# Two places for the weights in their buffers, by whether TensorE loads or streams them

## The chip, the cores and the metric

The kernel runs on one core of a Trainium2 chip. The metric is the device time of one execution in microseconds (us); several runs are taken and their median is told. One further execution was recorded by the hardware profiler, and the rows below come from it.

## What is computed

A trunk of two layers over 512 positions of 1024 channels, float32. Each layer: a normalisation, one input projection to 3072 columns that feeds three mixers (a gated linear recurrence in both directions, a two-dimensional Fourier transform, windowed attention with three dilations), one output projection with a residual, a second normalisation and an MLP with a squared ReLU and 4096 inner columns.

```
def reference(x, positions, attn_norm_w, w_in, hgrn_lower_bounds, w_out, mlp_norm_w, w_up, w_down, final_norm_w):
    ...
    for layer in range(DEPTH):
        h = rms_norm(x, attn_norm_w[layer])
        proj = h @ w_in[layer]
        a_q, a_i, a_zf, a_zb, a_g, b_u, c_q, c_k, c_v = jnp.split(proj, SPLIT_POINTS, axis=-1)
        ...
        mixed = jnp.concatenate([o_a, o_b, o_c], axis=-1)
        x = x + mixed @ w_out[layer]
        h = rms_norm(x, mlp_norm_w[layer])
        x = x + jnp.square(jax.nn.relu(h @ w_up[layer])) @ w_down[layer]
    return rms_norm(x, final_norm_w)
```

## The kernel before

**The dense products.** Every dense product is done in three passes over rounded halves. A float32 operand a is split into a high part ah (rounded to fewer bits, type fp32r) and the rest al; the product is ah·bh + ah·bl + al·bh (`mac3`, line 366). So each 128-row slice of the contraction costs three matmuls, each with its own load of a 128x128 stationary operand. In the profile such a matmul is two rows: a PEld LDWEIGHTS (the *loaded* operand, 128 columns per partition) and a PE MATMUL (the *streamed* operand, 512, 256 or 258 columns per partition). The load of the next matmul runs beside the streaming of the present one.

**Which operand is loaded.** In most products the weight is loaded and the activation streams, 512 columns at a time: the input projections `in…` through `proj_T` (line 439), the output projection `wo…`, the MLP's first product `up…` and, in layer 0, its second `dn…`. Where the result is wanted with positions on the partitions, the roles are turned round: the activation is loaded and the weight streams, 256 columns at a time (`proj_tok`, line 446). That holds for the weights of the recurrence's values (`in…_6`, `in…_7`), of the attention's values (`in…_18` to `in…_21`) and of the MLP's second product in layer 1 (`dt…`). The second Fourier step streams a constant matrix (`fc…`) in pieces of 258 columns against loaded activations.

**The weights.** `prefetch` (line 335) takes the next weight of a fixed list: SyncE's DMA brings 512 KB into a raw buffer, ScalarE rounds it into `wh` (line 351), VectorE subtracts for `wl` (line 352). For `fc` two DMAs of GpSimd's queue fill `wh` and `wl` directly. There are two buffers of each, 1152 float32 wide, of which 1024 (1032 for `fc`) are used, from the buffer's start.

**Where the operands lie.** The allocator places every pool's buffers one behind the other in a partition. All buffers that hold an operand of a dense matmul are multiples of 512 bytes long: `wh` and `wl` 4608, `xh` and `xl` (normalised activations) 16384, the pool `g` (MLP activations `ma`, mixer outputs `mix`, Fourier operands `fu` and `fab`) 4096. Each of them starts 32 bytes past a multiple of 512. A loaded operand is a slice of 128 columns, that is 512 bytes; slices start at multiples of 512 bytes from the buffer's start, streamed ones too. So the place of a loaded operand less that of a streamed one, modulo 512 bytes, is the same for all of these matmuls: 0. In this text that difference is called the *offset*. Two small groups differ. The first Fourier step streams its matrix `d` from a buffer that starts 192 bytes past a multiple of 512, against activations at 32: its offset is −160 (48 matmuls of 256 columns). The second step streams `fc` in pieces of 1032 bytes: its offsets are 0, −8, −16 and −24 in turn (96 matmuls of 258 columns).

**The order of the work.** The order of TensorE's instructions is written out: `ORDER` (line 38) gives, letter by letter, which stream issues next, and `weave` and `scripted` (lines 162 to 198) pin it; behind the end of that text a table of estimated clocks decides. In the MLPs and the output projections only one stream is left, and the matmuls follow one another.

Of the kernel before, what the change touches and what calls it, by code (L numbers as in the profile page):

```python
# [14 lines left out]
FR = mybir.dt.float32r  # L15
# [11 lines left out]
P = 128  # L27
# [10 lines left out]
ORDER = ("mr13mn7mng13mhmr6mhomh7mj6mhj4mhj7mhj9mhmj6m2hjh2mj4mh2mj2mh6mj2mh2mj6mj7mj5mj12mS3mS2T4mT2mT2mSVT2m3TVTST2m2T3mVS3T5mTVS4TVS2T2m2TVS2m2T2m2T2mVmTmT4mT2mT4mV35m",  # L38
         "11mnmn7mgmh6mh8moh9mh4mj3mj3mh3mjh6mjh4mj3mh9mj2h4mjmh6mh2mjmh6mj4mj4mj7mj6mj10mS6mS3m2T3mTmT2mVSTm2T3mTmVST4mTm2TVS4TVS4TSVTm3TmVS2m4T2mV3m2T5m2TmV40m")
HP = 400  # L40
RANK = "gonrxhjam"
DEEP = 2
START = "ho{}1"
# [76 lines left out]
class Trunk:  # L120
# [59 lines left out]
    def weave(self, streams, order=""):  # L180
# [4 lines left out]
        while live or self.fresh:  # L185
            for k in list(self.fresh):
                live[k] = [self.fresh.pop(k), 0.0]
            live = {k: live[k] for k in sorted(live, key=RANK.index)}
            times = {k: self.evt.get(w, 1e9) if isinstance(w, str) else w for k, (_, w) in live.items()}
# [123 lines left out]
    def weight_order(self):  # L313
# [18 lines left out]
                            o.append((w["w_dt"][hf, q, c], f"dt{l}_{hf}{q}{c}"))  # L332
        return o

    def prefetch(self, after=(None,)):
        nc = self.nc
        if not self.wlist:
            return
        src, name = self.wlist.pop(0)
        h = self.buf("wh", [P, 1152], f"wh_{name}", FR)  # L340
        l = self.buf("wl", [P, 1152], f"wl_{name}", FR)
        if isinstance(src, int):
            nc.gpsimd.dma_start(h[:, 0:4 * COLD], self.t["c_d2"][2 * src])
            nc.gpsimd.dma_start(l[:, 0:4 * COLD], self.t["c_d2"][2 * src + 1])
        else:
            raw = self.buf("wraw", [P, 1024], f"wr_{name}")
            n = 1024 // len(after)
            for i, then in enumerate(after):
                cs = slice(i * n, (i + 1) * n)
                nc.sync.dma_start(raw[:, cs], src[:, cs])  # L350
                nc.scalar.activation(h[:, cs], raw[:, cs], AF.Copy)  # L351
                nc.vector.tensor_tensor(l[:, cs], raw[:, cs], h[:, cs].bitcast(F32), op=OP.subtract)  # L352
                if then:
                    then()
        self.wnext.append((name, h, l))
# [122 lines left out]
    def hgrn_gates(self, layer, p, zq, zz):  # L478
# [4 lines left out]
        if p:  # L483
            yield f"kp{layer}0"
        with self.tc.high_priority(offset=HP):
            qn = self.buf("th", [P, S], f"hqn{layer}{p}")
# [56 lines left out]
    def hgrn_levels(self, layer, p):  # L543
# [25 lines left out]
        for lv in range(7):  # L569
# [26 lines left out]
            if lv > 0:  # L596
# [4 lines left out]
                te = tot.rearrange("p (n e) -> p n e", e=2)  # L601
            with self.tc.high_priority(offset=HP):
                for z, odd, lo in ((k, 0, 0), (k, 1, 64), (q, 1, 0), (q, 0, 64)):
# [368 lines left out]
    def mlp(self, layer):  # L972
# [7 lines left out]
        for half in range(2):  # L980
# [8 lines left out]
            if last:  # L989
# [7 lines left out]
                for q in range(4):  # L997
                    def ev(it, ps, q=q):
# [3 lines left out]
                        if half == 1:  # L1002
# [3 lines left out]
                            if q == 3:  # L1006
                                with self.tc.high_priority(offset=HP):
                                    r = self.final_scale(it, st)
# [132 lines left out]
```

## Time and profile before

| what | us |
|---|---|
| runs: median of 3 | 1297.52 |
| runs: lowest and highest | 1297.07, 1298.42 |
| profiled execution, its own time | 1296.64 |
| span of its instructions | 1294.9 |

The mean granted clock of TensorE over the span is 0.995 of its full 2.4 GHz. The profile gives times of instructions by engine: PE is the matmul, PEld the load of its stationary operand, DVE is VectorE, ACT ScalarE. A matmul's recorded duration holds the way of its last column through the array, so that successive matmuls overlap in the record; what one costs in a dense stretch is the distance from its start to the next one's start. It is got from a row that merges n matmuls: (length of the row less the duration of one) divided by n − 1, or from a piece of the chain of waits, whose length over its count gives it directly. In the chain, which is followed back from the last instruction, a piece is a stretch in which one engine's instructions set the end.

### The profile page before, as it was taken

To read this page: it belongs to the slowest core of one execution; us is meant where nothing else is said; L and a number is where in the kernel's file an instruction comes from. 1 tells how busy PE (TensorE), PEld (TensorE's weight loads), DVE (VectorE), ACT (ScalarE), POOL (GpSimd) and SP (SyncE) were. 2 spreads that over 40 slices of the span, in tenths; PEclk is the share of its full clock that TensorE was granted. 3 is DMA by queue.
4 is the path that set the end of the run, shared out by engine and by line. 5 is a ranking of instruction groups with operands and counts; after the bars stand their busy time and mean duration, and the time that the engine had idled before them with its cause. 6 is when DMAs were issued, how large, how long until landed. Compare 5 with 4: busy or idle time off the path is not lost.

```text
span 1294.9 us, 22041 instructions
## 1 busy us (share of the span) xinstructions
PE 1247.0 (96%) x9344; PEld 1071.1 (83%) x9344; DVE 705.0 (54%) x1314; ACT 538.2 (42%) x855; POOL 32.7 (3%) x54
## 2 busy tenths in 40 slices
PE   7799999899999999999999999889999999999997
PEld 6788877788888888888878987668888999888997
DVE  7798686554442234433369868765455322444234
ACT  6744265644442124433355335574344311344222
POOL 2100000000000000100010000000000000000000
PEclk9999999999999999999999999999999999999999
DMA  6321222142232222233322212304322232223221
GB/s 225 98 71 47 82 81 76 58 131 89 98 98 98 98 98 98 98 98 130 114 92 90 68 66 81 92 10 145 106 83 92 89 98 88 94 97 112 99 87 76
DMA packets 36498, 121.42 MB, mean 94 GB/s; under 512 B 4192, under 2 KB 5040, under 8 KB 36400
## 3 DMA queue, kind: packets, MB, share of 16 engines
q1 hardware_dynamic: 33120, 110.46, 25.8%
q0 software_dynamic: 2848, 7.98, 2.2%
q8 instruction: 73, 1.20, 0.4%
q10 hardware_dynamic: 432, 1.57, 0.3%
q14 instruction: 25, 0.20, 0.1%
HBM read 114.24 MB, written 4.72 MB: 92 GB/s over the span
## 4 chain that ended last, share of the span: by engine, by line
PE 85%; DVE 6%; ACT 5%; issue 2%; DMA 0%; SPq 0%; ACTq 0%; DVEq 0%
PE mm_up L144 27%; PE mt_dt L144 14%; PE md L144 13%; PE mm_in L144 11%; PE mo L144 7%; PE mt_cv L144 3%; PE ao L144 2%; PE at_tr L160 1%; PE sc L144 1%; ACT at L765 1%; PE mt_hi L144 1%; DVE hy L606 1%; ACT pt L779 1%; DVE wl_in L352 1%; PE f L144 1%
## 5 line engine op out<-in xcount | busy, mean ns | idle before, releaser
L144 PE MATMUL mt_dt<-wh_dt,ma 128*128 128x256 f32 x1024 | 144.3, 283 | 0.0
L144 PEld LDWEIGHTS mt_dt<-wh_dt,ma 128*128 128x128 f32 x1024 | 132.5, 192 | 0.2
L144 PE MATMUL mm_up<-xh,wl_up 128*128 128x512 f32 x512 | 130.1, 391 | 0.0
L965 DVE SCALAR_TENSOR_TENSOR mr<-mm_up,rb 128x512 f32<-128x512 f32 x64 | 44.1, 691 | 157.8 <-PE mm_up L144 149.9
L144 PE MATMUL mm_up<-xl,wh_up 128*128 128x512 f32 x512 | 129.7, 390 | 0.0
L144 PE MATMUL mm_up<-xh,wh_up 128*128 128x512 f32 x512 | 129.0, 390 | 0.0
L144 PE MATMUL md<-ma,wh_dn 128*128 128x512 f32 x512 | 121.3, 389 | 0.0
L351 ACT ACTIVATE wh_up<-wr_up 128x1024 fp32r<-128x1024 f32 x64 | 67.9, 1061 | 126.0 <-PE mm_up L144 100.8
L144 PEld LDWEIGHTS md<-ma,wh_dn 128*128 128x128 f32 x512 | 96.2, 188 | 19.9
L144 PEld LDWEIGHTS mm_up<-xh,wh_up 128*128 128x128 f32 x512 | 95.9, 188 | 19.8
L144 PEld LDWEIGHTS mm_up<-xl,wh_up 128*128 128x128 f32 x512 | 95.9, 188 | 19.7
L144 PEld LDWEIGHTS mm_up<-xh,wl_up 128*128 128x128 f32 x512 | 95.8, 188 | 19.7
L352 DVE TENSOR_TENSOR wl_dt<-wr_dt,wh_dt 128x1024 fp32r<-128x1024 f32 x32 | 39.2, 1224 | 98.6 <-ACT wh_dt L351 98.6
L352 DVE TENSOR_TENSOR wl_up<-wr_up,wh_up 128x1024 fp32r<-128x1024 f32 x64 | 78.0, 1218 | 21.4 <-ACT wh_up L351 19.1
L351 ACT ACTIVATE wh_dt<-wr_dt 128x1024 fp32r<-128x1024 f32 x32 | 33.9, 1060 | 124.1 <-PE mt_dt L144 101.3
L144 PE MATMUL mm_in<-xh,wh_in 128*128 128x512 f32 x288 | 77.8, 398 | 5.8 <-ACT xh L402 5.8
L144 PE MATMUL mt_dt<-wl_dt,ma 128*128 128x256 f32 x512 | 82.5, 283 | 0.0
L144 PE MATMUL mm_in<-xl,wh_in 128*128 128x512 f32 x288 | 78.2, 401 | 0.7 <-DVE xl L403 0.7
L351 ACT ACTIVATE wh_dn<-wr_dn 128x1024 fp32r<-128x1024 f32 x32 | 33.9, 1061 | 107.1 <-PE md L144 90.5
L967 ACT ACTIVATE mr<-mr 128x512 f32<-128x512 f32 x64 | 40.4, 632 | 88.4 <-DVE mr L965 88.3
L144 PE MATMUL mm_in<-xh,wl_in 128*128 128x512 f32 x288 | 76.3, 397 | 0.0
L144 PEld LDWEIGHTS mt_dt<-wl_dt,ma 128*128 128x128 f32 x512 | 70.8, 192 | 0.0
(229 smaller groups left out, 1988.3 us busy)
## 6 DMA issues: line engine op xcount, KB each, us to landing
wr_up<-in_w_up SPq DMA_DIRECT2D x64, 512.0 KB, 3.5
wr_in<-in_w_in SPq DMA_DIRECT2D x47, 512.0 KB, 3.5
wr_dn<-in_w_dn SPq DMA_DIRECT2D x32, 512.0 KB, 3.4
wr_dt<-in_w_dt SPq DMA_DIRECT2D x32, 512.0 KB, 3.5
wr_wo<-in_w_out SPq DMA_DIRECT2D x16, 512.0 KB, 3.7
wh_fc<-in_c_d POOLq DMA_DIRECT2D x4, 516.0 KB, 3.8
wl_fc<-in_c_d POOLq DMA_DIRECT2D x4, 516.0 KB, 4.3
x_in<-in_x SPq DMA_DIRECT2D x8, 256.0 KB, 5.7
```

Source lines behind the costliest of these rows:

```text
L144: return self.queue(self.nc.tensor.matmul(out, a, b, **kw))
L160: self.queue(self.nc.tensor.transpose(out, a, ident))
L351: nc.scalar.activation(h[:, cs], raw[:, cs], AF.Copy)
L352: nc.vector.tensor_tensor(l[:, cs], raw[:, cs], h[:, cs].bitcast(F32), op=OP.subtract)
L606: v.tensor_tensor(dst, dst, te[lo:lo + 64, :, 1 - odd, None].to_broadcast([64, nb, blk]), op=OP.mult)
L765: nc.scalar.activation(tt, tt, AF.Exp, bias=st4[:, 1:2], accum_out=st4[:, 2:3])
L779: nc.scalar.activation(pt, tr.rearrange("p (a b) -> p a b", b=P), AF.Copy)
L965: nc.vector.scalar_tensor_tensor(r, ps, 0.0, self.rb, op0=OP.max, op1=OP.mult)
L967: nc.scalar.activation(r, r, AF.Square)
```

## The change

A weight that TensorE streams is put 8 elements (32 bytes) behind its buffer's start, a weight that is loaded 120 elements (480 bytes). With buffers that start at 32 modulo 512, a loaded weight then starts at 0 modulo 512 and a streamed one at 64; the activations stay at 32. The offset becomes −32 for all dense matmuls that had 0, and −32, −40, −48 and −56 for the second Fourier step. The first Fourier step keeps −160.

```diff
 HP = 400
+PLACE = (120, 8)
 RANK = "gonrxhjam"
...
+    def streamed(self, name):
+        part, n = name.split("_")
+        return part[:2] in ("dt", "fc") or part[:2] == "in" and int(n) in (6, 7, 18, 19, 20, 21)
+
     def prefetch(self, after=(None,)):
         nc = self.nc
         if not self.wlist:
             return
         src, name = self.wlist.pop(0)
-        h = self.buf("wh", [P, 1152], f"wh_{name}", FR)
-        l = self.buf("wl", [P, 1152], f"wl_{name}", FR)
+        first = PLACE[self.streamed(name)]
+        h = self.buf("wh", [P, 1152], f"wh_{name}", FR)[:, first:]
+        l = self.buf("wl", [P, 1152], f"wl_{name}", FR)[:, first:]
```

The built programs of before and after hold the same 11,211 instructions in the same order on every engine, with the same waits and the same buffers at the same addresses. Only start addresses differ: of one operand in 5,760 less 48 matmuls that use a weight buffer, of the output of 193 roundings on ScalarE, of operands and output of 193 subtractions on VectorE, and of the targets of 8 DMAs of GpSimd's queue.

## Rows read from the trace of the kernel before

**Rows 1.** The page's busy times: engine, us, share of the span, instructions.
```profile
PE 1247.0 (96%) x9344; PEld 1071.1 (83%) x9344; DVE 705.0 (54%) x1314; ACT 538.2 (42%) x855; POOL 32.7 (3%) x54
```
**Rows 2.** The chain of waits: shares of the span by engine and line.
```profile
by line: PE mm_up L144 26.9%; PE mt_dt L144 14.2%; PE md L144 13.4%; PE mm_in L144 10.7%; PE mo L144 6.7%; PE mt_cv L144 3.4%; PE ao L144 2.1%; issue 1.9%; PE at_tr L160 1.3%; PE sc L144 1.1%; ACT at L765 1.0%; PE mt_hi L144 1.0%; DVE hy L6
```
**Rows 3.** Long pieces of that chain: start us, length us, what, count.
```profile
387.23 87.04 PE md L144 x384
...
1015.74 92.15 PE mt_dt L144 x768
```
**Rows 4.** Busy time of each engine in a stretch of layer 0's MLP.
```profile
345.00:530.00 185.00, 185.00 (x818) 153.28 (x817) 69.76 (x79) 58.90 (x71) 0.00 (x0) 1.00 0.29 97
```
**Rows 5.** Groups of matmuls and loads: shapes, count, busy us, mean ns, idle before.
```profile
L144 PE MATMUL mt_dt<-wh_dt,ma 128*128 128x256 f32 x1024 | 144.3, 283 | 0.0
...
L144 PE MATMUL mm_up<-xh,wl_up 128*128 128x512 f32 x512 | 130.1, 391 | 0.0
...
L144 PE MATMUL md<-ma,wh_dn 128*128 128x512 f32 x512 | 121.3, 389 | 0.0
...
L144 PE MATMUL mt_dt<-wl_dt,ma 128*128 128x256 f32 x512 | 82.5, 283 | 0.0
...
L144 PE MATMUL mm_in<-xh,wl_in 128*128 128x512 f32 x288 | 76.3, 397 | 0.0
...
L144 PE MATMUL md<-ma,wl_dn 128*128 128x512 f32 x256 | 63.2, 389 | 0.0
L144 PE MATMUL mo<-mix,wh_wo 128*128 128x512 f32 x256 | 63.2, 393 | 1.6 <-ACT mix L686 1.6
...
L144 PE MATMUL mo<-mix,wl_wo 128*128 128x512 f32 x128 | 32.6, 390 | 0.0
L144 PE MATMUL mt_cv<-wl_in,xh 128*128 128x256 f32 x128 | 21.6, 291 | 0.0
...
L144 PE MATMUL mt_hi<-wl_in,xh 128*128 128x256 f32 x64 | 11.1, 297 | 0.0
```
**Rows 6.** Timeline of PE in the first Fourier step (offset −160): start, length, what, count.
```profile
225.51 1.33 PE L144 MATMUL f<-d,fu 128*128 128x256 f32 x10
...
235.92 1.35 PE L144 MATMUL f<-d,fu 128*128 128x256 f32 x10
...
861.07 1.10 PE L144 MATMUL f<-d,fu 128*128 128x256 f32 x8
```
**Rows 7.** Timeline of PE in a short stretch of 256-column matmuls at offset 0.
```profile
688.87 0.64 PE L144 MATMUL mt_hi<-wh_in,xl 128*128 128x256 f32 x4
...
692.23 0.64 PE L144 MATMUL mt_hi<-wh_in,xh 128*128 128x256 f32 x4
```
**Rows 8.** All matmuls of the two Fourier steps: duration ns lowest, median, highest.
```profile
L144 PE MATMUL f<-wh_fc,fab x64: 277/283/388, 238.1 to 875.2; 128*128 128x258 f32 x64
L144 PE MATMUL f<-d,fu x48: 277/281/388, 225.3 to 862.1; 128*128 128x256 f32 x48
```
**Rows 9.** Timeline of PE in the second Fourier step (offsets 0 to −24).
```profile
871.08 1.15 PE L144 MATMUL f<-wh_fc,fab 128*128 128x258 f32 x8
...
873.41 1.12 PE L144 MATMUL f<-wh_fc,fab 128*128 128x258 f32 x8
```
**Rows 10.** Timeline of PE, transposes of 128 columns with a load each.
```profile
101.79 1.06 PE L160 MATMUL hk<-misc,hy 128*128 128x128 f32 x8 [1.58 <-DVE hy L606]
```
**Rows 11.** The same transposes: duration ns lowest, median, highest.
```profile
L160 PE MATMUL hk<-misc,hy x32: 272/273/328, 101.8 to 749.3; 128*128 128x128 f32 x32
```

## The prediction

> **What bounds the kernel now.** I read the busy times first: TensorE's matmul row is busy 1247 of 1294.9 us, VectorE 54%, ScalarE 42% [rows 1]. A matmul's recorded time overlaps the next one's, so this says only that TensorE is hardly ever without work. What sets the end is in the chain of waits: dense matmuls hold 26.9% (`mm_up`), 14.2% (`mt_dt`), 13.4% (`md`), 10.7% (`mm_in`), 6.7% (`mo`), 3.4% (`mt_cv`) and 1.0% (`mt_hi`) of the span, 76.3% together [rows 2]. In the MLP the other engines are far from it: in 185 us of layer 0, TensorE is busy throughout, VectorE for 69.76 us and ScalarE for 58.90 us [rows 4]. A dense matmul that becomes cheaper therefore shortens the kernel there one for one.
>
> What one matmul costs comes from two long pieces of the chain [rows 3]: 87.04 us for 384 matmuls of 512 columns is 226.67 ns each; 92.15 us for 768 of 256 columns is 119.99 ns each. The difference, 106.68 ns for 256 columns, is 0.4167 ns a column, one column per cycle at the full 2.4 GHz, which is also the clock granted there (1.00) [rows 4]. The streaming of 512 columns is thus 213.3 ns and that of 256 is 106.7 ns, and both leave the same rest: 13.3 ns per matmul, 32 cycles. This rest is all that a change of addresses can win where matmuls stand back to back. It doesn't grow with the columns streamed, so it belongs to the one load that each matmul has beside it.
>
> **The change part by part.** Nothing is moved, added or removed on any engine's queue; only start addresses change. There are four things to price.
>
> *The dense matmuls, offset 0 to −32.* First how many lie on the path. A share of the chain times 1294.9 us, over the cost of one, gives the matmuls that count:
> `mm_up` 348.3 us / 226.67 ns = 1537 (of 3 x 512 in [rows 5]);
> `md` 173.5 us = 765 (of 512 + 256); `mo` 86.8 us = 383 (of 256 + 128); `mm_in` 138.6 us = 611 (of 3 x 288).
> These have 512 columns: 3296. With 256 columns, at 119.99 ns: `mt_dt` 183.9 us = 1532 (of 1024 + 512), `mt_cv` 44.0 us = 367 (of 3 x 128), `mt_hi` 12.9 us = 108 (of 3 x 64): 2007. Together 5303. The rest of `mm_in`, `mt_cv` and `mt_hi` lies in the mixers beside chains of VectorE and ScalarE that end later, and I count nothing for it.
>
> Next what offset −32 does to one of them. No matmul of this kernel has that offset, so the trace bounds it by its neighbours. Offset −160, a multiple of 32 as −32 is: the first Fourier step, 256 columns. Three rows [rows 6] with a median duration of 281 ns [rows 8] give (1.33 − 0.28) / 9 = 117 ns, (1.35 − 0.28) / 9 = 119 ns and (1.10 − 0.28) / 7 = 117 ns; together 2.94 us over 25 steps, 117.6 ns: 2.4 ns under offset 0. That these stretches are short doesn't explain it: a stretch at offset 0 of about the same kind goes from 688.87 to 692.23 in 28 steps, 120.0 ns each [rows 7]. So the rest of 13.3 ns does depend on addresses, at least in part. Offsets 0 to −24 in turn, 258 columns: the second Fourier step. Its two rows [rows 9], with a median of 283 ns [rows 8], give (1.12 − 0.283) / 7 = 119.6 ns and (1.15 − 0.283) / 7 = 123.9 ns, where 258 columns with the rest of offset 0 would take 107.5 + 13.3 = 120.8. So there the rest is once 1.2 ns less and once 3.1 ns more. The bounds of the unknown are then: the whole 13.3 ns goes (what the load costs is gone entirely), or 3.1 ns are added. I take the value at −160, 2.4 ns, because it is the nearest row that shares its alignment to 32 bytes and has one offset throughout; the rows at −8 to −24 mix four offsets, two of which are odd multiples of 8. Sum: 5303 x 2.4 ns = 12.7 us less.
>
> The Trainium skill, page "TensorE: Matmul & The Clock Gate", section "Step-by-step: what each phase is for", speaks against any effect: it says that TensorE has two independent read ports into SBUF and that loading the next weights takes no read bandwidth from the running matmul. By it the placement would change nothing and the sum would be 0. The row at −160 doesn't agree with it, but it rests on 25 steps, so it stays a rival. The same page, section "Wait — 56ns, not 53.3ns?", gives the fixed cost of a matmul as about 2.5 ns over its columns; worked out from that page, an estimate, the sum would be 5303 x 10.8 ns = 57 us if nothing but that remained. The measured rest of 13.3 ns at offset 0 differs from it.
>
> *The roundings and subtractions* (lines 351 and 352) write and read at a shifted place, still a multiple of 32 bytes. The trace has no such operation at another shift. They lie beside TensorE's work in the MLP, with VectorE busy 38% and ScalarE 32% of the stretch [rows 4]: even a tenth more would stay covered. I take 0. Without the cover, a tenth of one rounding would be late once per buffer, which only the mixers could show.
>
> *The eight DMAs* into `wh` and `wl` for the Fourier matrix have the same sizes at another start; they are prefetched. I take 0.
>
> *The first Fourier step* keeps its offset and its time.
>
> What is late next: if each of the 24 matmuls on a weight became 13.3 ns faster, 5.44 us per weight would be 5.12 us; VectorE's and ScalarE's shares in [rows 4] would rise to 40% and 34%. No engine takes over.
>
> Against the profiled execution (1296.64 us, of which 1294.9 are the span) this gives 1283.9 us. The median of the runs lies 0.9 us above the profiled one, so as a median: 1297.5 − 12.7 = 1284.8 us.
>
> **The rivals.**
>
> *The conflict goes as a whole.* For: the rest is the same 13.3 ns at both widths, which looks like one collision of load and stream, and a collision that always begins in the same way at offset 0 can be moved off. Against: −160 removed a sixth of it. Price: 512 columns can win 13.3 ns, 3296 x 13.3 = 43.8 us. With 256 columns the load itself comes to bear: transposes of 128 columns, whose streaming is 53.3 ns, still follow one another at (1.06 − 0.27) / 7 = 113 ns [rows 10, 11], so I don't let 256 columns fall below 113: 2007 x 7 ns = 14.0 us. Sum 57.8 us: 1239.7 us.
>
> *Nothing happens.* The rest is a fixed cost of changing the stationary operand, and what −160 shows is the play of short stretches. For: the rest is 32 cycles at both widths, to the cycle. Against: [rows 6] beside [rows 7]. Time 1297.5, within 2.6 us.
>
> *Slower.* The collision settles at another, worse phase. The place is the back-to-back stretches of the MLPs; the price is that of the slower of the two rows of the second Fourier step, +3.1 ns: 5303 x 3.1 = 16.4 us, 1313.9 us. For: that row and its sister have the same program and the same addresses, so one offset can hold two phases, and one of them is dearer than offset 0. Against: the slow one appears only where offsets that aren't multiples of 16 stand in turn. It decides from +0.5 ns per matmul on, since 0.5 x 5303 = 2.6 us.
>
> That the change doesn't reach its aim can be left out: the addresses of the built program show −32 in every dense matmul but the 48 with −160 and the 96 of the second Fourier step.
>
> **How the numbers follow.** The bound of what a measurement of this kernel can tell from no change is 0.2%, 2.6 us. A part of the rest goes, 0.5 to 5 ns per matmul: 0.36; that alone would be 1271 to 1295 us. The whole or most of it goes, down to 1239.7: 0.27. Nothing, within 2.6 us: 0.15. Slower: 0.22. So faster is 0.63, same 0.15, slower 0.22. The range from 1240 to 1306 us leaves out the end of the whole gain and the dear half of the slower case, some 2 in 10 together: the upper end is +1.6 ns per matmul, half the price of the slower rival.
>
> **What would show it.** In the changed kernel the two long pieces of the chain are read again: 384 matmuls of 512 columns in 87.04 − 384 x 0.0024 = 86.1 us and 768 of 256 columns in 90.3 us would be right; 81.9 and 86.8 us the whole gain; the same lengths as before, no effect; longer ones the slower rival. The first Fourier step must stay at about 117.6 ns. The prediction is wrong in its sum, not only in its price, if those pieces get shorter and the span doesn't follow, since then a wait in the mixers or another engine has taken the place.

## The result: slower, two opposite effects of which the larger was missed

| runs | before, us | changed, us | ratio, 95% interval |
|---|---|---|---|
| median of 4 | 1297.97 | 1310.19 | 1.0092 [1.0074, 1.0109] |
| profiled execution, own time | 1296.64 | 1309.84 | |
| its span | 1294.9 | 1308.1 | |

The kernel became 12.2 us slower. The prediction was 12.7 us faster, and its range ended at 1306.

The chain of waits of the changed kernel has the same lines as before; its page gives the shares:

```profile
PE mm_up L145 27%; PE mt_dt L145 14%; PE md L145 14%; PE mm_in L145 10%; PE mo L145 7%; PE mt_cv L145 3%; PE ao L145 2%; PE at_tr L161 1%; DVE hx L612 1%; DVE hy L612 1%; DVE wl_in L358 1%; PE sc L145 1%; ACT at L771 1%; PE mt_hi L145 1%; ACT pt L785 1%
```

Its long pieces (start us, length us, what, count) answer to [rows 3]:

```profile
298.12 7.93 PE mm_up L145 x34
...
389.49 89.60 PE md L145 x384
...
568.69 89.60 PE md L145 x384
...
936.72 7.93 PE mm_up L145 x34
...
1031.54 89.60 PE mt_dt L145 x768
```

The two kinds of matmul went opposite ways. 384 matmuls of 512 columns take 89.60 us where they took 87.04: 233.33 ns each, 6.67 ns or 16 cycles more. 768 matmuls of 256 columns take 89.60 us where they took 92.15: 116.67 ns each, 3.33 ns or 8 cycles less. The matching pieces of the chain before, for the bounds of the stages:

```profile
298.31 7.71 PE mm_up L144 x34
...
561.31 87.04 PE md L144 x384
648.35 8.16 PE mm_in L144 x36
...
922.95 7.71 PE mm_up L144 x34
```

So the first mixers and output projection end at 298.12 against 298.31. Layer 0's MLP takes 568.69 + 89.60 − 298.12 = 360.17 us against 648.35 − 298.31 = 350.04: 10.1 us more, which is its 1536 matmuls of 512 columns at 6.67 ns (10.2). Layer 1's mixers and output projection take 278.43 against 274.60 us, 3.8 more. From there to the end of the span it is 371.4 against 371.95 us: 768 matmuls at +6.67 ns (5.1 us) and 1536 at −3.33 ns (5.1 us) cancel.

The two mixer stages also differ by TensorE's granted clock. In the rows below, busy times of the engines in a stretch as in [rows 4], the third figure from the end is the granted share of 2.4 GHz: first the two mixer stages of the kernel before, then those of the changed kernel.

```profile
0.00:298.30 298.30, 271.53 (x2729) 227.52 (x2730) 217.14 (x492) 159.00 (x282) 16.74 (x30) 0.98 0.30 97
...
648.40:922.90 274.50, 261.14 (x2713) 220.05 (x2712) 199.40 (x429) 139.08 (x253) 9.47 (x14) 1.00 0.26 83
...
0.00:298.10 298.10, 271.46 (x2729) 224.07 (x2730) 217.00 (x492) 159.32 (x282) 16.81 (x30) 0.99 0.30 97
...
658.30:936.70 278.40, 265.58 (x2713) 220.84 (x2713) 199.43 (x429) 139.21 (x253) 9.72 (x14) 0.99 0.26 82
```

Taken stretch by stretch, the kernel before spends 10.2 us of layer 0's stage at the lower level of 1.2 GHz and none of layer 1's; the changed kernel spends 6.8 and 3.4 us there. The totals are equal, so the sum of the two stages isn't touched. But 3.4 us at half the clock hold back up to 1.7 us of matmuls (an estimate), which makes the change look that much better in layer 0's mixers and that much worse in layer 1's.

The operations that write at the shifted place kept their pace. The rounding and the subtraction of an `up` weight take 1062 and 1218 ns there, where they took 1061 and 1218:

```profile
L358 DVE TENSOR_TENSOR wl_up<-wr_up,wh_up 128x1024 fp32r<-128x1024 f32 x64 | 77.9, 1218 | 21.9 <-ACT wh_up L357 19.5 <-PE mm_up L145 2.5
...
L357 ACT ACTIVATE wh_up<-wr_up 128x1024 fp32r<-128x1024 f32 x64 | 67.9, 1062 | 132.2 <-PE mm_up L145 106.5 <-PE mt_dt L145 9.1 <-PE md L145 9.1
```

### The profile page after: what moved, and what is told of

It is laid out like the page before. It is cut to its first block, busy times and chain, and to the rows that moved or that the text cites. A ratio compares the mean times of both kernels' runs of the same rounds, so it can differ in the third digit from the quotient of the medians.

```text
span 1308.1 us, 22041 instructions
## 1 busy us (share of the span) xinstructions
PE 1260.9 (96%) x9344; PEld 1062.5 (81%) x9344; DVE 704.8 (54%) x1314; ACT 539.1 (41%) x855; POOL 33.1 (3%) x54
## 4 chain that ended last, share of the span: by engine, by line
PE 84%; DVE 8%; ACT 5%; issue 2%; DMA 0%; SPq 0%; ACTq 0%; DVEq 0%
PE mm_up L145 27%; PE mt_dt L145 14%; PE md L145 14%; PE mm_in L145 10%; PE mo L145 7%; PE mt_cv L145 3%; PE ao L145 2%; PE at_tr L161 1%; DVE hx L612 1%; DVE hy L612 1%; DVE wl_in L358 1%; PE sc L145 1%; ACT at L771 1%; PE mt_hi L145 1%; ACT pt L785 1%
## 5 line engine op out<-in xcount | busy, mean ns | idle before, releaser
L145 PE MATMUL mt_dt<-wh_dt,ma 128*128 128x256 f32 x1024 | 140.5, 279 | 0.0
L145 PE MATMUL mm_up<-xh,wl_up 128*128 128x512 f32 x512 | 133.1, 396 | 0.0
L145 PE MATMUL mm_up<-xl,wh_up 128*128 128x512 f32 x512 | 132.8, 396 | 0.0
L145 PE MATMUL mm_up<-xh,wh_up 128*128 128x512 f32 x512 | 132.1, 395 | 0.0
L145 PEld LDWEIGHTS mt_dt<-wh_dt,ma 128*128 128x128 f32 x1024 | 128.8, 188 | 0.2
L145 PE MATMUL md<-ma,wh_dn 128*128 128x512 f32 x512 | 124.6, 395 | 0.0
L357 ACT ACTIVATE wh_up<-wr_up 128x1024 fp32r<-128x1024 f32 x64 | 67.9, 1062 | 132.2 <-PE mm_up L145 106.5
L358 DVE TENSOR_TENSOR wl_up<-wr_up,wh_up 128x1024 fp32r<-128x1024 f32 x64 | 77.9, 1218 | 21.9 <-ACT wh_up L357 19.5
L357 ACT ACTIVATE wh_dn<-wr_dn 128x1024 fp32r<-128x1024 f32 x32 | 34.0, 1062 | 111.6 <-PE md L145 93.9
L357 ACT ACTIVATE wh_in<-wr_in 128x1024 fp32r<-128x1024 f32 (+1 forms) x49 | 50.9, 1039 | 47.9 <-PE mm_in L145 18.2
```

What stands on the lines that cost most here:

```text
L145: return self.queue(self.nc.tensor.matmul(out, a, b, **kw))
```

## The experiments

The theory after the result: what a matmul costs over its columns hangs on the offset and on how many columns stream. (The sweeps will show that these two alone don't fix it.) Its rivals were that the place of the loaded operand itself counts, that the role counts (weight or activation loaded), that the shifted writes of ScalarE and VectorE cost the time, and that the cost is a fixed one of changing the stationary operand.

### One part of the change at a time

```diff
-PLACE = (120, 8)
+PLACE = (0, 8)      # e1: streamed weights alone
+PLACE = (120, 0)    # e2: loaded weights alone
```

> Only the weights that are streamed (256 and 258 columns) are moved, 8 elements up; loaded weights stay at their buffers' start, so 512 columns keep offset 0. Width theory (the price hangs on the offset and on how many columns stream): mt_dt 116.67 ns each as in the changed kernel, md and mm_up back at 226.67 ns; some 2007 matmuls on the path times 3.3 ns, about 6.5 us less than before, 1291 us. Rival (the shifted writes of ScalarE and VectorE cost the time, or the loss is spread over both): slower than 1297.5 us, with md above 226.67 ns.

> Only the weights that are loaded are moved, 120 elements up; streamed ones stay at the start. Width theory: md and mm_up 233.33 ns, mt_dt 119.99 ns; 3296 matmuls on the path times 6.67 ns, 22 us more than before less what the mixers hide, 1315 to 1320 us; with the streamed-only kernel's gain it must add up to the changed kernel's 12.2 us loss within 2 us. Rival (both moves are needed for the loss): under 1310 us.

Against a median of 1298.15 us of before on the same chip, streamed alone gave 1290.65 us (ratio 0.9937 [0.9922, 0.9952]) and loaded alone 1318.33 us (1.0152 [1.0131, 1.0173]): −7.5 and +20.2, together +12.7, where the whole change made +12.2. The chain's pieces, streamed alone:

```profile
386.47 87.04 PE md L145 x384
...
1015.26 89.60 PE mt_dt L145 x768
```

Loaded alone:

```profile
394.46 89.60 PE md L145 x384
...
1037.93 92.15 PE mt_dt L145 x768
```

Each half of the change moves its own kind of matmul by the steps seen in the whole, and leaves the other kind at its price of before. The shifted writes alone are out as the cause: both kernels have them, and one got faster.

### The other operand moved

The weights stay at their buffers' start and `xh`, `xl` go 32 bytes up, so that `mm_up` has offset −32 with its loaded operand at 32, not 0, modulo 512.

```diff
-        xh = self.buf("xh", [P, KT, S], f"xh{which}{layer}", FR)
-        xl = self.buf("xl", [P, KT, S], f"xl{which}{layer}", FR)
+        xh, xl = (self.buf(tag, [P, KT * S + 128], f"{tag}{which}{layer}", FR)[:, 8:8 + KT * S]
+                  .rearrange("p (k s) -> p k s", k=KT) for tag in ("xh", "xl"))
```

> The weights stay at their buffers' start, and the normalised activations xh and xl are put 32 bytes up instead: the offset of in and up is -32 again, but now the loaded operand starts at 32 and the streamed one at 64 modulo 512; dn, wo and dt have offset 0; where xh is loaded (hi, cv) the offset is +32. Relation theory (only the difference of the two places counts): mm_up 233.33 ns, md 226.67 ns, mt_dt 119.99 ns. Place theory (the loaded operand's own start at 0 modulo 512 is what costs): mm_up 226.67 ns or less. Time by the relation theory about 1297.5 + (1537 + 611) x 6.67 ns = 1312 us less what the mixers hide.

```profile
389.65 87.06 PE md L145 x384
476.72 89.60 PE mm_up L145 x384
...
1025.00 92.16 PE mt_dt L145 x768
```

`mm_up` costs 233.33 ns, `md` and `mt_dt` what they did before; the single run took 1308.46 us, 1312 less what the mixers hide. At this offset the difference of the two places counts, not either place.

### All places

Each weight of the MLPs got a place of its own, first in steps of 16 bytes, then the 4-byte places between.

```diff
-        first = PLACE[self.streamed(name)]
+        first = self.place(name)    # e3: up0 n//2*8, up1 n//2, dn0 4+8*i, dt1 0, 8 ... 120 and 4, 12 ... 124
+                                    # e6: the places between, from lists
```

> Each weight of the MLPs gets its own place: loaded up weights of layer 0 at offsets 0, 32 ... 480 bytes (two weights each), loaded dn weights at 16, 48 ... 496, loaded up weights of layer 1 at 0, 4 ... 60, streamed dt weights at offsets 0, -16, -32 ... -496. Width theory: 512 columns give 226.67 ns at 0 and 233.33 near 480 (= -32), 256 columns 119.99 at 0 and 116.67 at -32; between these the cost moves in steps of whole cycles, and some offset is cheaper than both kernels have. Collision at the start theory: only a few offsets near 0 differ, the rest are alike and lower than 226.67 and 119.99. Fixed-cost theory for 512 columns: all offsets but a few lie within 1 ns of 226.67.

> The 4-byte places that the first sweep left out: 512 columns at offsets 68 to 300 bytes that aren't multiples of 16, 256 columns at offsets -36 to -200 that aren't. If the price has a period of 256 bytes, as the first sweep's rows at 0 and 256, 16 and 272 had it, offsets 260, 264, 268 repeat those of 4, 8, 12 (232.4, 230.6, 233.4 ns). Collision theory with a width of 16 bytes: 512 columns stay dear (over 228 ns) everywhere but near 0, 16, 256, 272, and 256 columns have a trough near -112 (first sweep: 113.3 ns settled) a few places wide. If there is a cheaper place for 512 columns than 226.67 ns, it is among these.

Timeline of PE in the first sweep, 512 columns: the tile from 393.29 (its second weight; offset 16), then from 398.74 offset 48; at 576.59 offset 304 begins.

```profile
393.29 3.79 PE L145 MATMUL md<-ma,wh_dn 128*128 128x512 f32 x16
...
398.74 3.90 PE L145 MATMUL md<-ma,wh_dn 128*128 128x512 f32 x16
...
404.34 3.90 PE L145 MATMUL md<-ma,wh_dn 128*128 128x512 f32 x16
...
576.59 3.90 PE L145 MATMUL md<-ma,wh_dn 128*128 128x512 f32 x16
...
582.19 1.10 PE L145 MATMUL md<-ma,wh_dn 128*128 128x512 f32 x4
```

The 24 matmuls from 393.29 to 398.74 take 227 ns each, those from 398.74 to 404.34 take 233.3, and at offset 304 = 256 + 48 from 576.59 to 582.19 again 233.3. Streamed weights of 256 columns at offset −112:

```profile
1225.92 0.61 PE L145 MATMUL mt_dt<-wl_dt,ma 128*128 128x256 f32 x4
1226.37 1.07 PE L145 MATMUL mt_dt<-wh_dt,ma 128*128 128x256 f32 x8
1227.28 0.61 PE L145 MATMUL mt_dt<-wl_dt,ma 128*128 128x256 f32 x4
1227.73 1.07 PE L145 MATMUL mt_dt<-wh_dt,ma 128*128 128x256 f32 x8
1228.64 0.61 PE L145 MATMUL mt_dt<-wl_dt,ma 128*128 128x256 f32 x4
```

From 1225.92 to 1228.64 are 24 matmuls, 113.3 ns each. Worked out in the same way from the starts of successive matmuls of each weight, the first six left out (ns a matmul, loaded less streamed place modulo 256 bytes):

```
offset         0    16    32    48    64    80    96   112   128   144   160   176   192   208   224   240
512 columns 226.7 226.7 233.3 233.3 233.3 232.0 234.3 233.3 232.4 233.4 233.3 230.1 228.9 231.8 233.3 228.4
256 columns 120.0 117.1 118.3 119.3 117.8 119.3 118.6 118.7 118.7 114.1 119.9 118.4 117.8 118.4 117.8 118.7
```

Of the 512-column prices, every one at a multiple of 16 was read again 256 bytes further and agreed within 0.1 ns (48 and 304 above). Of the 256-column ones fourteen were read twice in the same way: twelve agreed within 0.3 ns (144 and 400 with 114.1 and 114.0), while 176 read 120.0 and 118.4 and 240 read 118.7 and 117.6. (The second readings of 16 and 48 come from a tile in which two weights take turns.) Some prices lie on whole steps of 8 cycles, 3.33 ns; others don't, such as 235.0 ns at 28, which is 52 cycles over the columns.

Over all 64 places of a period, 512 columns never fell under 226.67 ns; they reached it at 0 and 16 and at a few odd places (120, 132, 156, 204, 252) and stood as high as 236.6 at 212 and 237.2 at 164. Before lay in the trough of the wide matmuls by its layout. For 256 columns the odd places were tried from −36 to −200 only; they gave 116.7 to 122.8 ns, and the only deep place that was found is 144, which is −112.

An offset and a width don't fix the price, though: one offset can hold two settled rhythms. In layer 1 of the first sweep two successive weights lie at offset 16, the first up to 986.3, the second from there on:

```profile
984.75 1.98 PE L145 MATMUL mm_up<-xh,wl_up 128*128 128x512 f32 x8
...
988.88 2.03 PE L145 MATMUL mm_up<-xl,wh_up 128*128 128x512 f32 x8
```

With 0.39 us for one matmul [rows 5], the first row gives 227 ns and the second 234; the starts of single matmuls give 226.7 and 233.3. Each stretch follows four transposes, and the dear rhythm holds for 18 matmuls, until the next ones interrupt it. For 256 columns at −32 the sweep gave 117.8 ns (224 in the table) where the changed kernel's long pieces gave 116.67; the sweep's steps repeat from early on, so this too is a second rhythm and not a stretch that was too short to settle. What selects the rhythm isn't shown.

Of the expectations, "some offset is cheaper than both kernels have" held for 256 columns and failed for 512; the collision at the start fell, since offsets far from 0 are dear as well, and so did the fixed cost for 512 columns. Of the second sweep's, 512 columns were to be cheap near 0 and 16 only, and aren't; the trough at −112 was to be a few places wide, and −108 and −116 read 120.0 and 122.6. The repeat of 4, 8, 12 at 260, 264, 268 held at two of three (232.4, 230.8, and 230.0 for 233.4); of six further odd places read 256 bytes apart (20 to 44) five agreed within 0.1 ns, and 36 read 234.6 and 233.4.

### The best of both

```diff
-PLACE = (120, 8)
+PLACE = (0, 28)
```

> Loaded weights stay at their buffers' start (offset 0, 226.67 ns for 512 columns, the lowest that the first sweep found); streamed weights lie 28 elements up, offset -112, where the first sweep settled at 113.3 ns for 256 columns. Relation theory: 2007 matmuls on the path times 6.67 ns, 13.4 us less than before, 1284 to 1286 us. If the trough was a transient of a short stretch, mt_dt settles at 117 ns or more and the time is 1291 us or more.

1285.12 us against 1299.64 of before on that chip, ratio 0.9909 [0.9891, 0.9926]: 14.5 us less, for 13.4 expected. The chain's pieces:

```profile
384.90 87.04 PE md L145 x384
...
1013.60 87.08 PE mt_dt L145 x768
```

87.08 us for 768 is 113.4 ns; the trough is no transient. This version is about 1% faster than before, and the interval leaves out 1.

### Width or role, and how width enters

In layer 0's second product, where weights are loaded, odd tiles stream their columns in two matmuls of 256 (e5), or the tiles stream 512, 480 ... 288 columns (e9); first half of the MLP at offset 0, second at −32.

```diff
+                self.mm(out[:, 0:256], a, b[:, 0:256], start=start and i == 0, stop=last, skip_group_check=True)
+                self.mm(out[:, 256:512], a, b[:, 256:512], start=False, stop=last, skip_group_check=True)
...
+                    n = 512 - 32 * m
...
+                        yield from self.mac3(ps[:, 0:n], [(h[:, k * P:(k + 1) * P], l[:, k * P:(k + 1) * P], a[8 * c + k][:, 0, 0:n], a[8 * c + k][:, 1, 0:n])
```

> In layer 0's second MLP product every odd output tile streams its 512 columns as two matmuls of 256 with the same loaded weight each; first half of the MLP at offset 0, second half at -32. Relation theory (offset and streamed columns set the price, not whether a weight or an activation is loaded): 119.99 ns each at offset 0, 116.67 ns at -32, while the even tiles give 226.67 and 233.33 ns. Role theory (loaded weights are dear at -32, loaded activations cheap): the split ones at -32 stay over 120 ns. If the second of the two matmuls needed no load, a pair would cost one rest instead of two.

> In layer 0's second MLP product the eight output tiles stream 512, 480, 448, 416, 384, 352, 320 and 288 columns (the other columns of that product are left out); first half of the MLP at offset 0, second half at -32. If width is what turns the sign of -32, the rest over the streamed columns goes at -32 from 20 ns at 512 columns to near 10 ns at 288 with a change of order somewhere between, and stays 13.3 ns at offset 0. If the collision only happens while the load runs, in the first 107 ns, width can't matter at all and 288 columns have the same rest as 512 at either offset.

Timeline of PE with halves, offset 0 at 402.27, offset −32 at 582.90:

```profile
402.27 4.00 PE L146 MATMUL md<-ma,wh_dn 128*128 128x256 f32 x32
406.11 2.08 PE L146 MATMUL md<-ma,wl_dn 128*128 128x256 f32 x16
...
582.90 2.03 PE L146 MATMUL md<-ma,wl_dn 128*128 128x256 f32 x16
584.77 3.89 PE L146 MATMUL md<-ma,wh_dn 128*128 128x512 f32 x16
588.50 2.03 PE L146 MATMUL md<-ma,wl_dn 128*128 128x512 f32 x8
...
595.97 3.93 PE L146 MATMUL md<-ma,wh_dn 128*128 128x256 f32 x32
599.74 0.52 PE L146 MATMUL md<-ma,wl_dn 128*128 128x256 f32 x3
```

At offset 0 the halves cost 3.84 / 32 = 120.0 ns. At −32 they cost 1.87 / 16 = 116.9 ns with the weight loaded, beside whole tiles at 233.1; the split tile from 595.97 keeps to the other rhythm, 3.77 / 32 = 117.8 ns. Each half has a load of its own, and a pair pays two rests. So the width sets the sign and the role doesn't.

Timeline of PE with the widths, 480 columns at offset 0, then 352 at −32:

```profile
397.65 3.63 PE L145 MATMUL md<-ma,wh_dn 128*128 128x480 f32 x16
...
402.85 3.63 PE L145 MATMUL md<-ma,wh_dn 128*128 128x480 f32 x16
...
592.76 2.72 PE L145 MATMUL md<-ma,wh_dn 128*128 128x352 f32 x16
...
596.60 2.72 PE L145 MATMUL md<-ma,wh_dn 128*128 128x352 f32 x16
```

That is 5.20 / 24 = 216.7 ns, 40 cycles over the 480 columns, and 3.84 / 24 = 160.0 ns, 32 cycles over the 352. All widths, worked out from the starts (cycles of 0.4167 ns over one per column):

```
columns      288   320   352   384   416   448   480   512
offset 0      28    32    35    32    36    39    40    32
offset -32    32    32    32    40    48    48    48    48
```

At −32 the rest rises from 32 to 48 cycles near 400 columns. At offset 0 it wanders from 28 to 40; that it is 32 at both 256 and 512 columns is no law of the widths. Two expectations failed: the rest doesn't stay at 13.3 ns at offset 0, and 288 columns at −32, which were to have some 10 ns, have 13.3 ns, more than the 10 ns of 256 columns.

### What the rest is paid for

Three runs, all at a place of layer 0's second product or of its whole MLP, with the layout of before where nothing else is said. In e8 odd tiles load one column repeated (first half) or stream one column repeated (second half); in e11 they load 64 columns (first half) or 32 (second half) and leave the other output rows out; in e10 the passes take turns so that the offset alternates.

```diff
+                    a = a[:, 0:1].to_broadcast([P, P])                     # e8, first half
+                    b = b[:, 0:1].to_broadcast([P, S])                     # e8, second half
...
+                self.mm(out[0:w], a[:, 0:w], b, start=start and i == 0, stop=last, skip_group_check=True)   # e11
...
+            seq = [s for ah, al, bh, bl in triples for s in ((ah, bh), (al, bh))] + [(ah, bl) for ah, al, bh, bl in triples]   # e10
```

> Layout of before, offset 0. In layer 0's second MLP product, odd output tiles: in the first half of the MLP the loaded operand is one column repeated 128 times, in the second half the streamed operand is one column repeated 512 times, so that one of the two reads stands still at one place (these products are left out of the result so). Read theory (the rest over the streamed columns comes from the two reads walking through the same parts of SBUF): the rest differs from 13.3 ns in both halves, and falls by more than half where the collision can't recur. Fixed-cost theory (changing the stationary operand costs 13.3 ns): 226.67 ns in both halves as in the even tiles.

> Layout of before, offset 0. In layer 0's second MLP product, odd output tiles load only 64 columns per matmul in the first half of the MLP and 32 in the second, and stream 512 as before (the other output rows of these tiles are left out). If the 13.3 ns over the streamed columns is paid for the load's reads, it falls with the columns loaded: about 8 ns (221 ns each) at 64 and 5 ns (218 ns) at 32, given that 2.5 ns remained when the streamed operand stood still. If the lowest rest that any offset gave (32 cycles at 512 columns, 16 at 256) is the stream's own walk through SBUF, it stays at 13.3 ns, 226.67 ns each, at both.

> In layer 0's MLP the passes ah.bh and al.bh take turns, slice by slice, and wl lies elsewhere than wh (wh at the buffer's start, wl 0, 16 ... 240 bytes up for dn, 8, 24 ... 248 for up), so that the offset changes from one matmul to the next. If the cost is a state that settles at a fixed offset, a changing offset gives pairs between the two single prices or off them, and some pair may fall under 226.67 ns a matmul; if each load is priced by its own offset alone, every pair costs the mean of 226.67 and the price that the sweeps found for wl's offset, so never under 226.67.

Timeline of PE with one operand standing still, the loaded one at 404.06, the streamed one at 578.75:

```profile
404.06 2.01 PE L146 MATMUL md<-ma,wl_dn 128*128 128x512 f32 x8
...
409.61 2.01 PE L146 MATMUL md<-ma,wl_dn 128*128 128x512 f32 x8
...
578.75 1.89 PE L146 MATMUL md<-ma,wl_dn 128*128 128x512 f32 x8
580.47 3.62 PE L146 MATMUL md<-ma,wh_dn 128*128 128x512 f32 x16
583.93 1.89 PE L146 MATMUL md<-ma,wl_dn 128*128 128x512 f32 x8
585.65 3.80 PE L146 MATMUL md<-ma,wh_dn 128*128 128x512 f32 x16
```

With the loaded operand still, 231.2 ns from 404.06 to 409.61. With the streamed one still, (585.65 − 578.75) / 32 = 215.6 ns by these rounded rows; by the starts of the tile's single matmuls it is 215.8 ns, 2.5 ns over the 213.3 of its columns. A fixed cost of changing the stationary operand is therefore at most that, and the other 10.8 ns at offset 0 are paid only where the stream walks through SBUF. The Trainium skill, page "TensorE: Matmul & The Clock Gate", section "Wait — 56ns, not 53.3ns?", gives the fixed part as about 2.5 ns; this row agrees. The same page of the Trainium skill, section "Step-by-step: what each phase is for", has load and stream read through two ports that don't disturb each other; the runs here disagree, since the place of the loaded operand alone moved 512 columns between 226.7 and 237.2 ns.

Timeline of PE with loads of 64 columns up to 406.59, and of 32 from 570.27 to 581.39:

```profile
404.75 2.01 PE L146 MATMUL md<-ma,wl_dn 128*64 128x512 f32 x8
406.59 3.79 PE L146 MATMUL md<-ma,wh_dn 128*128 128x512 f32 x16
410.22 1.98 PE L146 MATMUL md<-ma,wl_dn 128*128 128x512 f32 x8
...
570.27 3.87 PE L146 MATMUL md<-ma,wh_dn 128*32 128x512 f32 x16
...
581.39 0.86 PE L146 MATMUL md<-ma,wh_dn 128*128 128x512 f32 x3
```

Shorter loads did not help. Over 188 steps each within these tiles, loads of 64 columns gave 230.0 ns a matmul ((406.59 − 404.75) / 8 in the rows) and of 32 columns 231.6, against 227.0 for whole loads in the same run. Both expectations failed: the rest neither falls with the load nor stays at 13.3 ns. Alternating offsets, with the first six matmuls of each weight left out, gave 226.6 to 236.2 ns over 32 pairs, seven of them (0 with itself among these) at 226.6 to 226.7 and none lower; the prices aren't the mean of the two single ones (0 with 32 gave 234.8 where the mean is 230.0). So as far as these runs go a load has no price of its own; load and stream settle into a rhythm together, and its cost is read, not computed.

## Why the prediction was wrong

**What bounds the kernel** was right: a dense matmul's price goes through to the end. The count on the path was good too: 3296 x 6.67 − 2007 x 3.33 = 22.0 − 6.7 = 15.3 us, with the measured prices, against 13.2 between the two profiled executions. Of the missing 2 us some 1.4 lie in the mixers and output projections (994 x 6.67 − 475 x 3.33 = 5.0 us counted, 3.6 measured) and 0.6 in the last stage. That layer 0's mixers ended at the same time in spite of dearer matmuls can in part be the granted clock: the kernel before was 3.4 us longer at 1.2 GHz there, up to 1.7 us of matmuls.

**The step that failed** is the price: "I take the value at −160, 2.4 ns", put on all 5303 matmuls. It was measured on 256 columns, and for those it was near (3.33 ns), which is in part luck: nothing ties −160 to −32, and the sweep gave 118.6 ns at −160, 1.4 ns under offset 0. For 512 columns no row of before had any offset but 0, and the sign there is the other one. What misled was the sentence that the rest "doesn't grow with the columns streamed, so it belongs to the one load": two equal rests at one offset, taken for a law. e9 shows 28 to 40 cycles at the widths between, and e11 shows that the rest doesn't follow the load.

**The rivals.** The slower one had the mechanism, a worse settled state, but one price for both widths, +3.1 ns; it was +6.67 and −3.33. Its time of 1313.9 us came near the measured 1310.2 by the cancelling of these two, which is luck. Its place held for layer 0's MLP alone, where the loss is 10.1 us; in layer 1's MLP the two signs cancel. Its remark that one offset can hold two phases was borne out in the sweep. The whole gain is refuted for 512 columns over all 64 places; for 256 columns it is nearly there at −112, at the 113 ns that the prediction took as a bound from the transposes [rows 10]. That the same thing sets both isn't shown. "Nothing happens" fell with e1 and e2.

**Priced at nothing**: the roundings and subtractions kept their durations, as predicted. The first Fourier step kept its offset and its time: its first twelve matmuls take 1.65 us where they took 1.66. No engine took over.

**Open.** Why the cost has a period of 256 bytes, why it rises with width at −32, what the stream meets on its walk when only 32 columns are loaded, and what selects one of two rhythms at an offset: the runs bound this but don't name it. A matmul without any load beside it was not tried.

## What to carry to other kernels

Where two operands are read side by side, price their places separately for each shape that streams, and don't carry a price from one shape to another, even if both cost the same at the present place. One run with a different place for each weight gives a first map, since a place's price shows in a few dozen matmuls of the timeline. A place can have two prices, so the best one is read again in long stretches. Then move only the operands that gain: here the streamed weights alone, 28 elements up.

## What the runs showed of the hardware beyond that

At 2.4 GHz (granted clock 1.00 in these stretches) back-to-back matmuls settle at 16 to 57 cycles over their columns, often on whole steps of 8 (16, 24, 32, 40, 48 were all seen) but not always (28, 35 and 52 were seen too). The place of the loaded operand against the streamed one, modulo 256 bytes, moved a matmul of 512 columns from 226.7 to 237.2 ns and one of 256 columns from 113.3 to 122.8 ns. In one stretch at half the clock no rest shows: in the changed kernel, at a granted clock of 0.50 from 877.5 to 880.5 us, the last seven of eight matmuls of 258 columns start 214 or 218 ns apart, and 258 columns alone take 215 ns at 1.2 GHz.
